# Decoder trunk on one core: rotation and key stacking rearranged, softmax from negated scores, probabilities scaled by a scalar per row

## The chip, the cores and the metric

The kernel runs on one core of one Trainium2 chip. The metric is the device time of one execution in microseconds; lower is better. The profile is one execution of the same program, recorded by the hardware profiler; its times are microseconds from its first instruction.

## What is computed

Two layers of a decoder trunk over 256 positions of width 1024, all in float32. Each layer is a half-step SwiGLU, a token mixer, and another half-step SwiGLU; a final RMSNorm ends it.

```
for l in range(2):
    x = x + 0.5 * swiglu(rms_norm(x, norm_ffn1[l]), ...)      # 1024 -> 2816 -> 1024
    x = x + hybrid_mixer(rms_norm(x, norm_mix[l]), ...)
    x = x + 0.5 * swiglu(rms_norm(x, norm_ffn2[l]), ...)
return rms_norm(x, norm_final)
```

The mixer has 8 NSA heads (in two groups that share keys; compressed, selected and window branches, which at 256 positions come to one causal softmax with two gates and one softmax over 15 compressed blocks) and 8 MoBA heads (one causal softmax each). Heads are 64 wide. Queries and keys get a partial rotation of their first 16 dimensions, and every softmax is masked, has its row maximum subtracted and its sum clamped at one:

```
x1 * cos - x2 * sin,  x2 * cos + x1 * sin                       # partial rotation
p = exp(s - max(s)); p / maximum(sum(p), 1.0)                   # masked softmax, s = q.k / 8
```

## The kernel before

Every weight block (128 x 1024) is streamed from HBM in the order of its use. Because the products are made of rounded float32 parts, each block is split in two: `whi`, a rounding copy on ScalarE (line 254), and `wlo`, the remainder, a subtraction on VectorE (line 283). Five raw and seven split buffers let this run ahead of TensorE; `st.pump()` and `st.split()` are the places in the program at which further blocks are split. Products are three matmuls (high by high, high by low, low by high).

The work is written out as one long program by hand, phase by phase: feed-forward, mixer, feed-forward, twice. Inside the mixer the order of calls (`m_feat("mk", 0)`, `nsa_s(0)`, `c_hidden()`, ...) interleaves three things: projections of MoBA keys, queries and values, NSA attention, and MoBA attention with the output projection. A scheduler then fixes the order on each engine from the program's order and its own estimates; at run time every engine goes through its queue in that fixed order and waits on semaphores.

The steps that the change touches, with their lines:

- Rotation. `rope_begin` (759) copies a projection from PSUM to SBUF on ScalarE (762), has ScalarE's queue issue two DMAs that bring the partner rows over into `SW` (763, 764; 16 rows each), and multiplies the projection by the cosines on VectorE (765). `rope_end` (767) multiplies `SW` by the signed sines and adds it to the result, both on GpSimd (768, 769). Both run seven times in a mixer: three times for NSA (queries, keys, queries), four times for MoBA.
- Key stacks. `stack_k` (798) and `m_stack` (1078) write a key's high part (ScalarE, 802 and 1086) and low part (VectorE, 803 and 1087) on 64 partitions; `repeat_k` (805) and `m_repeat` (1090) copy both to the other 64 partitions by DMAs from ScalarE's queue (807, 1093), two for NSA and four for MoBA in each mixer. `nsa_s` (1026) and `moba_s` (1188) need all 128 partitions.
- Softmax. `softmax` (976) scales, masks and takes the row maximum of scores in one VectorE instruction each (984, 985), negates the maxima (986), and lets ScalarE take the exponential with the sum (988, 989). `normalize` (992) works out the factor of each row on VectorE (994 to 998) and multiplies the probabilities by it on GpSimd (1000, 1001), with the factor read as a broadcast tensor.
- Values. The gates and the NSA values are evicted by ScalarE (1118, 1122), as are the MoBA values (1112), which `m_v` does after the last of its `st.pump()` calls; the four output accumulators (`out_block`, 1180; matmuls at 539 to 541) take over PSUM banks of tag `A`, which the MoBA values must leave first.

Of the kernel before, what the change touches and what calls it, by code (L numbers as in the profile page):

```python
# [133 lines left out]
def constants():  # L134
# [6 lines left out]
    for h in range(2):  # L141
        for d in range(half):
            C[h * 64 + 8 * d] = C[h * 64 + 8 * d + 4] = cos[:, d]
            Sg[h * 64 + 8 * d] = -sin[:, d]
            Sg[h * 64 + 8 * d + 4] = sin[:, d]
# [165 lines left out]
def trunk(ctx, tc, xin, wst, w1st, gains, glast, cst, small, out, phases=PHASES, n_raw=5, n_hl=7):  # L311
# [435 lines left out]
    def mixer(pi, l):  # L747
# [93 lines left out]
        rotk = rawk[:, 2:4]  # L841
        rs = state["rs"]
        rs8 = mp.tile([128, 2], F32, name="rs8", bufs=2)
        nrs = mp.tile([128, 2], F32, name="nrs", bufs=2)
        G.tensor_scalar(rs8, rs, DH ** -0.5, None, op0=OP.mult)
        G.tensor_scalar(nrs, rs, -1.0, None, op0=OP.mult)
        rope_begin(b1, rawq[:, 0:2], SW[:, 0:2], rotq[:, 0:2], con("C"))
# [21 lines left out]
        rope_begin(b2, rawk[:, 0:2], SW[:, 2:4], rotk, CK)  # L869
# [3 lines left out]
        rope_end(SW[:, 0:2], rotq[:, 0:2], con("Sg"))  # L873
# [4 lines left out]
        rope_begin(b3, rawq[:, 2:4], SW[:, 0:2], rotq[:, 2:4], con("C"))  # L878
        rope_end(SW[:, 2:4], rotk, SK)
# [3 lines left out]
        rope_end(SW[:, 0:2], rotq[:, 2:4], con("Sg"))  # L883
        repeat_k()
# [91 lines left out]
        def softmax(key, s1, s0, nb, gates):  # L976

            P = mp.tile([128, 3, 2, 128], F32, name="P", tag="P", bufs=3)[:, :, :nb]
            m = mp.tile([128, 2, nb], F32, name=f"mx{nb}", bufs=3)
# [3 lines left out]
            for r in range(nb):  # L983
                V.tensor_tensor_reduce(P[:, 0:2, r], s1[:, :, r], mk, rs8[:, 1:2], -3e38, OP.add, OP.max, m[:, 0, r:r + 1])
                V.tensor_tensor_reduce(P[:, 2, r], s0[:, r], m0, rs8[:, 0:1], -3e38, OP.add, OP.max, m[:, 1, r:r + 1])
            V.tensor_scalar(nm, m, -1.0, None, op0=OP.mult)
            for r in range(nb):
                A.activation(P[:, 0:2, r], P[:, 0:2, r], AF.Exp, bias=nm[:, 0, r:r + 1], accum_out=sm[:, 0, r:r + 1])
                A.activation(P[:, 2, r], P[:, 2, r], AF.Exp, bias=nm[:, 1, r:r + 1], accum_out=sm[:, 1, r:r + 1])
            PR[key] = (P, sm, nb, gates)  # L990

        def normalize(key):
# [63 lines left out]
        cur, ends, stacks, reps = {}, [], [], []  # L1056

        def m_feat(which, i):
# [5 lines left out]
            if i % 2 == 1:  # L1064
                h = i // 2
                raw = mp.tile([128, 2, S], F32, name="mraw", tag="F", bufs=2)
                tabs = (CK, SK) if which == "mk" else (con("C"), con("Sg"))
                sw, ro = SW[:, 2 * h:2 * h + 2], cur["rot"][:, 2 * h:2 * h + 2]
                rope_begin(cur["b"], raw, sw, ro, tabs[0])
# [264 lines left out]
```

## Time and profile before

| | |
|---|---|
| median of 3 runs | 1039.81 us (1039.14 to 1040.87) |
| the profiled execution's own time | 1037.38 us |
| its span, first to last instruction | 1035.6 us |
| TensorE busy | 1000.6 us (97%), 5861 matmuls |
| VectorE busy | 688.5 us (66%) |
| ScalarE busy | 593.3 us (57%) |
| GpSimd busy | 326.1 us (31%) |

1.8 us of the profiled execution's time lie outside its span. Engine names in the profile: PE is TensorE's matmul, PEld its weight load, DVE VectorE, ACT ScalarE, POOL GpSimd; a q behind an engine's name is its queue. The two mixers lie at about 197 to 340 us and 705 to 849 us. A matmul's end is modelled, so that neighbouring matmuls overlap in the records.

### The profile page before, as it was taken

The page shows a single profiled execution, that of the slowest core. Times are in us where ns is not written, and L with a number is a line of the kernel's source. Part 1 is how long each engine was busy: PE and PEld are TensorE (multiplying, and loading weights), DVE is VectorE, ACT ScalarE, POOL GpSimd, SP SyncE. Part 2 cuts the span into 40 slices and gives each one's busy share as a digit, 9 for nine tenths or more (in the row PEclk, how much of TensorE's full clock was granted, in tenths as well). Part 3 has the DMA queues.
Part 4 walks back from the last instruction along what each step waited for, and adds up shares of the span by engine and source line. Part 5 has one row for each costly group of instructions (what it writes and reads, how often), then busy time and mean ns, then how long its engine had stood idle before and what let it go on. Part 6 is the DMA issues. An engine that isn't in the chain of part 4 may idle for free.

```text
span 1035.6 us, 16186 instructions
## 1 busy us (share of the span) xinstructions
PE 1000.6 (97%) x5861; PEld 861.0 (83%) x5861; DVE 688.5 (66%) x1187; ACT 593.3 (57%) x1137; POOL 326.1 (31%) x425
## 2 busy tenths in 40 slices
PE   9999999998998999999999999999999989999997
PEld 7788888898776888888888888889888778888885
DVE  6766666589865766566676666566986648666664
ACT  6745555457766655555565555545677747555552
POOL 3622232145641422222232223121475313222230
PEclk9999999999999999999999999999999999999999
DMA  8685776455444466666556677764543426666531
GB/s 268 241 279 186 274 240 218 145 171 157 114 126 125 154 198 196 188 197 186 163 182 203 186 234 239 262 196 138 181 131 108 143 82 208 194 209 193 193 122 41
DMA packets 52848, 188.21 MB, mean 182 GB/s; under 512 B 6368, under 2 KB 6496, under 8 KB 51616
## 3 DMA queue, kind: packets, MB, share of 16 engines
q1 hardware_dynamic: 49680, 182.04, 55.4%
q10 hardware_dynamic: 3088, 5.14, 2.0%
q8 instruction: 46, 0.75, 0.3%
q14 instruction: 34, 0.28, 0.1%
HBM read 182.04 MB, written 1.05 MB: 177 GB/s over the span
## 4 chain that ended last, share of the span: by engine, by line
PE 83%; DVE 7%; ACT 5%; issue 2%; DMA 2%; POOL 1%; ACTq 0%; POOLq 0%; DVEq 0%
PE psB L560 15%; PE psA L539 9%; PE psA L540 9%; PE psA L541 9%; PE psB L562 8%; PE psD L560 8%; PE psC L560 7%; PE psD L562 4%; PE psC L562 4%; DVE wlo L283 3%; PE psA L533 2%; PE psA L532 2%; PE psA L534 2%; ACT whi L254 1%; PE psA L398 1%
## 5 line engine op out<-in xcount | busy, mean ns | idle before, releaser
L283 DVE TENSOR_TENSOR wlo<-wraw,whi 128x1024 fp32r<-128x1024 f32 x325 | 408.2, 1259 | 242.1 <-ACT whi L254 240.5
L254 ACT CAST whi<-wraw 128x1024 fp32r<-128x1024 f32 (+1 forms) x326 | 339.5, 1044 | 304.2 <-issue 175.4
L560 PE MATMUL psB<-x,whi 128*128 128x512 f32 x688 | 243.1, 394 | 3.4 <-DVE hs L627 3.3
L635 POOL TENSOR_TENSOR hs<-hs,rbc 128x256 f32<-128x256 f32 x88 | 75.0, 853 | 380.3 <-DVE hs L627 364.6
L562 PE MATMUL psB<-x,wlo 128*128 128x256 f32 x688 | 192.5, 280 | 0.0
L560 PEld LDWEIGHTS psB<-x,whi 128*128 128x128 f32 x688 | 129.2, 188 | 32.5 <-DVE hs L627 4.3
L541 PE MATMUL psA<-wlo,hp 128*128 128x512 f32 x352 | 136.9, 389 | 0.0
L540 PE MATMUL psA<-whi,hp 128*128 128x512 f32 x352 | 136.8, 389 | 0.0
L539 PE MATMUL psA<-whi,hp 128*128 128x512 f32 x352 | 136.2, 390 | 0.0
L562 PEld LDWEIGHTS psB<-x,wlo 128*128 128x128 f32 x688 | 129.4, 188 | 1.4
L637 POOL TENSOR_TENSOR hs<-hs,rbc 128x256 f32<-128x256 f32 x88 | 102.9, 1170 | 80.5 <-ACT hs L636 80.5
L560 PE MATMUL psC<-x,whi 128*128 128x512 f32 x352 | 124.9, 392 | 0.0
L560 PE MATMUL psD<-x,whi 128*128 128x512 f32 x352 | 124.8, 392 | 0.0
L562 PE MATMUL psC<-x,wlo 128*128 128x256 f32 x352 | 98.6, 280 | 0.9 <-DVE wlo L283 0.9
L562 PE MATMUL psD<-x,wlo 128*128 128x256 f32 x352 | 98.4, 280 | 0.0
L560 PEld LDWEIGHTS psC<-x,whi 128*128 128x128 f32 x352 | 66.1, 188 | 14.5
L560 PEld LDWEIGHTS psD<-x,whi 128*128 128x128 f32 x352 | 66.1, 188 | 14.4
L541 PEld LDWEIGHTS psA<-wlo,hp 128*128 128x128 f32 x352 | 66.1, 188 | 13.9
L539 PEld LDWEIGHTS psA<-whi,hp 128*128 128x128 f32 x352 | 66.0, 188 | 13.7
L540 PEld LDWEIGHTS psA<-whi,hp 128*128 128x128 f32 x352 | 66.1, 188 | 12.3
L532 PE MATMUL psA<-x,whi 128*128 128x256 f32 x256 | 72.8, 284 | 1.2 <-ACT PT L1010 0.8
L533 PE MATMUL psA<-x,whi 128*128 128x256 f32 x256 | 72.3, 283 | 0.7 <-DVE x L380 0.7
(229 smaller groups left out, 1586.3 us busy)
## 6 DMA issues: line engine op xcount, KB each, us to landing
wraw<-in_w SPq DMA_DIRECT2D x318, 512.0 KB, 4.3
W1a<-in_w SPq DMA_DIRECT2D x4, 1024.0 KB, 6.3
W1mixn<-in_w SPq DMA_DIRECT2D x2, 1024.0 KB, 7.6
W1late<-in_w SPq DMA_DIRECT2D x2, 1024.0 KB, 6.5
KM<-KM ACTq DMA_DIRECT2D x8, 256.0 KB, 3.2
wraw<-in_w SPq DMA_DIRECT2D x4, 420.0 KB, 3.7
wraw<-in_w SPq DMA_DIRECT2D x4, 256.0 KB, 5.1
X<-in_small SPq DMA_DIRECT2D x1, 1024.0 KB, 9.5
```

What stands on the lines that cost most here:

```text
L254: self.last_hi = self.nc.scalar.copy(hi[:, a:b], raw[:, a:b]).ins
L283: eng.tensor_sub(lo[:, :c], raw[:, :c], hi[:, :c].bitcast(F32))
L532: T.matmul(o, hi, xh, start=first, stop=False, skip_group_check=True)
L533: T.matmul(o, hi, xl, start=False, stop=False, skip_group_check=True)
L534: T.matmul(o, lo, xh, start=False, stop=last, skip_group_check=True)
L539: T.matmul(o, parts[:, 0, c], hi, start=first, stop=False, skip_group_check=True)
L540: T.matmul(o, parts[:, 1, c], hi, start=False, stop=False, skip_group_check=True)
L541: T.matmul(o, parts[:, 0, c], lo, start=False, stop=last, skip_group_check=True)
L560: T.matmul(o, blk128(hi, k), x.rearrange("p a t -> p (a t)"), start=k == 0, stop=k == KT - 1, skip_group_check=True)
L562: T.matmul(o[:, S:], blk128(lo, k), x[:, 0], start=False, stop=k == KT - 1, skip_group_check=True)
L635: G.tensor_mul(g, g, state["rbc"])
L637: G.tensor_mul(g, g, state["rbc5"])
```

## The change

1. The exponent's scale becomes -1 and the scores are scaled by the negative factor `nrs8` (a new tiny GpSimd instruction), so that the reduction is a minimum and gives the negated maximum; the instruction of line 986 goes.
2. The sine table changes sign and is applied before the rows are swapped: VectorE multiplies the projection by it from PSUM into `other`, the two DMAs swap rows of `other`, and `rope_end` is one addition on VectorE. The copy by ScalarE stays only for the two NSA query rotations of a mixer, whose unrotated queries are needed later, and comes behind the DMAs.
3. The key stacks are written to both halves of the partitions by ScalarE and VectorE; the six DMAs of a mixer and their calls go.
4. `normalize` uses an instruction with one tensor and a scalar per row on GpSimd.
5. One of the two evictions of NSA values and of MoBA values moves to VectorE, and those of MoBA come ahead of the last `st.pump()`.

```diff
-            Sg[h * 64 + 8 * d] = -sin[:, d]
-            Sg[h * 64 + 8 * d + 4] = sin[:, d]
+            Sg[h * 64 + 8 * d] = sin[:, d]
+            Sg[h * 64 + 8 * d + 4] = -sin[:, d]
...
-        def rope_begin(b, raw, sw, ro, ctab):
+        def rope_begin(b, raw, other, sw, ro, tabs):
             src = b.rearrange("p (a t) -> p a t", a=2)
-            A.copy(raw, src)
-            A.dma_start(sw[0:128:8], raw[4:128:8])
-            A.dma_start(sw[4:128:8], raw[0:128:8])
-            V.tensor_mul(ro, src, ctab[:, None, :].to_broadcast([128, 2, S]))
-
-        def rope_end(sw, ro, stab):
-            G.tensor_mul(sw, sw, stab[:, None, :].to_broadcast([128, 2, S]))
-            G.tensor_add(ro, ro, sw)
+            ctab, stab = (t[:, None, :].to_broadcast([128, 2, S]) for t in tabs)
+            V.tensor_mul(other, src, stab)
+            A.dma_start(sw[0:128:8], other[4:128:8])
+            A.dma_start(sw[4:128:8], other[0:128:8])
+            V.tensor_mul(ro, src, ctab)
+            if raw is not None:
+                A.copy(raw, src)
+
+        def rope_end(sw, ro):
+            V.tensor_add(ro, ro, sw)
...
                 src = rotk[half[g]].rearrange("p a (b t) -> p b a t", b=2)
-                A.copy(KK[g][half[g], 0], src)
-                V.tensor_sub(KK[g][half[g], 1], src, KK[g][half[g], 0].bitcast(F32))
-
-        def repeat_k():
-            for g in range(2):
-                A.dma_start(KK[g][half[1 - g]].bitcast(F32), KK[g][half[g]].bitcast(F32))
+                own = KK[g][half[g], 0]
+                for r in (half[g], half[1 - g]):
+                    A.copy(KK[g][r, 0], src)
+                for r in (half[g], half[1 - g]):
+                    V.tensor_sub(KK[g][r, 1], src, own.bitcast(F32))
...
-            m = mp.tile([128, 2, nb], F32, name=f"mx{nb}", bufs=3)
...
-                V.tensor_tensor_reduce(P[:, 0:2, r], s1[:, :, r], mk, rs8[:, 1:2], -3e38, OP.add, OP.max, m[:, 0, r:r + 1])
-                V.tensor_tensor_reduce(P[:, 2, r], s0[:, r], m0, rs8[:, 0:1], -3e38, OP.add, OP.max, m[:, 1, r:r + 1])
-            V.tensor_scalar(nm, m, -1.0, None, op0=OP.mult)
+                V.tensor_tensor_reduce(P[:, 0:2, r], s1[:, :, r], mk, nrs8[:, 1:2], 3e38, OP.add, OP.min, nm[:, 0, r:r + 1])
+                V.tensor_tensor_reduce(P[:, 2, r], s0[:, r], m0, nrs8[:, 0:1], 3e38, OP.add, OP.min, nm[:, 1, r:r + 1])
...
-                A.activation(P[:, 0:2, r], P[:, 0:2, r], AF.Exp, bias=nm[:, 0, r:r + 1], accum_out=sm[:, 0, r:r + 1])
+                A.activation(P[:, 0:2, r], P[:, 0:2, r], AF.Exp, scale=-1.0, bias=nm[:, 0, r:r + 1], accum_out=sm[:, 0, r:r + 1])
...
-                G.tensor_mul(P[:, 0:2, r], P[:, 0:2, r], sm[:, 0, r:r + 1, None].to_broadcast([128, 2, 128]))
-                G.tensor_mul(P[:, 2, r], P[:, 2, r], sm[:, 1, r:r + 1].to_broadcast([128, 128]))
+                G.tensor_scalar(P[:, 0:2, r], P[:, 0:2, r], sm[:, 0, r:r + 1], None, op0=OP.mult)
+                G.tensor_scalar(P[:, 2, r], P[:, 2, r], sm[:, 1, r:r + 1], None, op0=OP.mult)
...
             for a in range(2):
-                A.copy(K[half[a], :, a, 0], ro[half[a]])
-                V.tensor_sub(K[half[a], :, a, 1], ro[half[a]], K[half[a], :, a, 0].bitcast(F32))
-            reps.append(K)
-
-        def m_repeat():
-            K = reps.pop(0)
-            for a in range(2):
-                A.dma_start(K[half[1 - a], :, a].bitcast(F32), K[half[a], :, a].bitcast(F32))
+                own = K[half[a], :, a, 0]
+                for r in (half[a], half[1 - a]):
+                    A.copy(K[r, :, a, 0], ro[half[a]])
+                for r in (half[a], half[1 - a]):
+                    V.tensor_sub(K[r, :, a, 1], ro[half[a]], own.bitcast(F32))
...
+            if i == 3:
+                A.activation(MV[:, 0], cur["vb"][0], AF.Copy, scale=rs[:, 0:1])
+                V.tensor_scalar(MV[:, 1], cur["vb"][1], rs[:, 1:2], None, op0=OP.mult)
             st.pump()
-            if i == 3:
-                for blk in range(2):
-                    A.activation(MV[:, blk], cur["vb"][blk], AF.Copy, scale=rs[:, blk:blk + 1])
...
-        for blk in range(2):
-            A.activation(VN[:, blk], vb[blk][:, :S], AF.Copy, scale=rs[:, blk:blk + 1])
+        A.activation(VN[:, 0], vb[0][:, :S], AF.Copy, scale=rs[:, 0:1])
+        V.tensor_scalar(VN[:, 1], vb[1][:, :S], rs[:, 1:2], None, op0=OP.mult)
```

## Rows read from the trace of the kernel before

**Rows 1.** The page, section 4: the chain that ended last, by engine.

```profile
PE 83%; DVE 7%; ACT 5%; issue 2%; DMA 2%; POOL 1%; ACTq 0%; POOLq 0%; DVEq 0%
```

**Rows 2.** Stretches of mixer 1: length, busy us (instructions) per engine, clock, DMA.

```profile
214.00:237.00 23.00, 21.49 (x209) 19.50 (x209) 22.21 (x26) 13.55 (x23) 11.73 (x8) 1.00 0.62 184
237.00:268.00 31.00, 28.44 (x220) 25.57 (x219) 26.60 (x88) 22.27 (x67) 21.24 (x30) 1.00 0.51 149
268.00:297.00 29.00, 26.86 (x181) 22.69 (x179) 20.96 (x60) 22.38 (x61) 17.82 (x28) 1.00 0.35 97
```

**Rows 3.** Waits of TensorE, whole span: total us, times, longest us.

```profile
PE psA L539 <- ACT late L1112: 3.4, 2, 1.8
...
PE psB L1031 <- DVE qs L778: 2.8, 2, 1.5
...
PE psD L1048 <- ACT PcT L969: 2.1, 2, 1.0
PE psB L1031 <- DVE mx L984: 2.0, 2, 1.0
```

**Rows 4.** Key stack's DMAs (tile view), and ScalarE's timeline behind them.

```profile
DMA to landing us min/median/max: 4.9/5.3/5.4
...
231.18 2.19 ACTq L807 DMA_DIRECT2D KK<-KK  x2
233.41 0.41 ACT L776 CAST qs<-rotq 64x256 fp32r<-64x256 f32 x1 [2.48 <-DVE KK L803]
```

**Rows 5.** VectorE, 199 to 345 us, groups by form: busy us, mean ns, idle before.

```profile
L986 DVE TENSOR_SCALAR nm<-mx 128x4 f32<-128x4 f32 x8 | 3.1, 384 | 0.1
L803 DVE TENSOR_TENSOR KK<-rawk,KK 64x512 fp32r<-64x512 f32 x2 | 2.9, 1425 | 0.0
...
L765 DVE TENSOR_TENSOR rotq<-psA,const 128x512 f32<-128x512 f32 x2 | 1.4, 683 | 0.0
...
L283 DVE TENSOR_TENSOR wlo<-wraw,whi 128x560 fp32r<-128x560 f32 x1 | 0.7, 734 | 0.0
```

**Rows 6.** VectorE's timeline: two subtractions with GpSimd's rotation beside them, and without.

```profile
219.01 4.27 DVE L283 TENSOR_TENSOR wlo<-wraw,whi 128x1024 fp32r<-128x1024 f32 x2
...
227.09 2.36 DVE L283 TENSOR_TENSOR wlo<-wraw,whi 128x1024 fp32r<-128x1024 f32 x2
```

**Rows 7.** Busy us (instructions) in mixer 1: GpSimd's line 768, then line 769.

```profile
197.00:345.00 148.00, 10.71 (x7) 1.00 0.45 134
...
197.00:345.00 148.00, 11.25 (x7) 1.00 0.45 134
```

**Rows 8.** GpSimd, 199 to 345 us, groups by form; line 902 (ns min/median/max).

```profile
L1000 POOL TENSOR_TENSOR P<-P,sm 128x256 f32<-128x256 f32 x24 | 17.1, 712 | 29.0 <-DVE sm L996 16.2 <-DVE sm L998 4.3 <-ACT P L988 3.9
L1001 POOL TENSOR_TENSOR P<-P,sm 128x128 f32<-128x128 f32 x24 | 16.2, 677 | 0.0
...
L902 POOL TENSOR_SCALAR hxt<-hxt x2: 298/298/298, 240.6 to 749.2; 128x128 f32<-128x128 f32 x2
```

**Rows 9.** Who waited for the negated maxima (us, times), and one such wait.

```profile
  ACT P L988: 18.3, 13
...
264.25 0.51 ACT L988 ACTIVATE P<-P,nm 128x256 f32<-128x256 f32 x1 [3.47 <-DVE nm L986]
```

**Rows 10.** ScalarE's timeline at the MoBA values, and TensorE's first output matmul.

```profile
295.37 1.03 ACT L254 CAST whi<-wraw 128x1024 fp32r<-128x1024 f32 x1
296.30 0.68 ACT L1112 ACTIVATE late<-psA,ny 128x512 f32<-128x512 f32 x1
...
297.03 0.50 PE L539 MATMUL psA<-whi,mixn 128*128 128x512 f32 x1 [1.76 <-ACT late L1112]
```

**Rows 11.** Swapped rows: who waited for them (us, times), and the DMAs' landing.

```profile
  POOL SW L768: 24.7, 11
...
DMA to landing us min/median/max: 1.7/1.9/5.9
```

**Rows 12.** ScalarE, 199 to 345 us, groups by form: the copy of line 762.

```profile
L762 ACT COPY mraw<-psA 128x512 f32<-128x512 f32 x4 | 2.3, 576 | 0.0
```

More of the change, by code (lines that the diff above doesn't have):

```diff
@@ L840, in mixer @@
         rawq, rotq, rawk = RW("rawq"), RW("rotq"), RW("rawk")
-        rotk = rawk[:, 2:4]
+        other, rotk = rawk[:, 0:2], rawk[:, 2:4]
         rs = state["rs"]
         rs8 = mp.tile([128, 2], F32, name="rs8", bufs=2)
+        nrs8 = mp.tile([128, 2], F32, name="nrs8", bufs=2)
         nrs = mp.tile([128, 2], F32, name="nrs", bufs=2)
         G.tensor_scalar(rs8, rs, DH ** -0.5, None, op0=OP.mult)
+        G.tensor_scalar(nrs8, rs, -DH ** -0.5, None, op0=OP.mult)
         G.tensor_scalar(nrs, rs, -1.0, None, op0=OP.mult)
-        rope_begin(b1, rawq[:, 0:2], SW[:, 0:2], rotq[:, 0:2], con("C"))
+        rope_begin(b1, rawq[:, 0:2], other, SW[:, 0:2], rotq[:, 0:2], (con("C"), con("Sg")))
         st.pump()
@@ L868, in mixer @@
                     V.tensor_mul(Fk[kv][par * 64:(par + 1) * 64, :, g * NC_:(g + 1) * NC_], blocks(src), blocks(rb))
-        rope_begin(b2, rawk[:, 0:2], SW[:, 2:4], rotk, CK)
+        rope_begin(b2, None, other, SW[:, 2:4], rotk, (CK, SK))
         st.pump()
@@ L872, in mixer @@
         feature_one(b3[:, :S], st.use("in", l, 2), True)
-        rope_end(SW[:, 0:2], rotq[:, 0:2], con("Sg"))
+        rope_end(SW[:, 0:2], rotq[:, 0:2])
         for r in (0, 1):
@@ L877, in mixer @@
         feature_one(b3[:, S:], st.use("in", l, 3), False)
-        rope_begin(b3, rawq[:, 2:4], SW[:, 0:2], rotq[:, 2:4], con("C"))
-        rope_end(SW[:, 2:4], rotk, SK)
+        rope_begin(b3, rawq[:, 2:4], other, SW[:, 0:2], rotq[:, 2:4], (con("C"), con("Sg")))
+        rope_end(SW[:, 2:4], rotk)
         stack_k()
@@ L882, in mixer @@
         nsa_v(0)
-        rope_end(SW[:, 0:2], rotq[:, 2:4], con("Sg"))
-        repeat_k()
+        rope_end(SW[:, 0:2], rotq[:, 2:4])
         nsa_v(1)
@@ L983, in softmax @@
             for r in range(nb):
-                V.tensor_tensor_reduce(P[:, 0:2, r], s1[:, :, r], mk, rs8[:, 1:2], -3e38, OP.add, OP.max, m[:, 0, r:r + 1])
-                V.tensor_tensor_reduce(P[:, 2, r], s0[:, r], m0, rs8[:, 0:1], -3e38, OP.add, OP.max, m[:, 1, r:r + 1])
-            V.tensor_scalar(nm, m, -1.0, None, op0=OP.mult)
+                V.tensor_tensor_reduce(P[:, 0:2, r], s1[:, :, r], mk, nrs8[:, 1:2], 3e38, OP.add, OP.min, nm[:, 0, r:r + 1])
+                V.tensor_tensor_reduce(P[:, 2, r], s0[:, r], m0, nrs8[:, 0:1], 3e38, OP.add, OP.min, nm[:, 1, r:r + 1])
             for r in range(nb):
-                A.activation(P[:, 0:2, r], P[:, 0:2, r], AF.Exp, bias=nm[:, 0, r:r + 1], accum_out=sm[:, 0, r:r + 1])
-                A.activation(P[:, 2, r], P[:, 2, r], AF.Exp, bias=nm[:, 1, r:r + 1], accum_out=sm[:, 1, r:r + 1])
+                A.activation(P[:, 0:2, r], P[:, 0:2, r], AF.Exp, scale=-1.0, bias=nm[:, 0, r:r + 1], accum_out=sm[:, 0, r:r + 1])
+                A.activation(P[:, 2, r], P[:, 2, r], AF.Exp, scale=-1.0, bias=nm[:, 1, r:r + 1], accum_out=sm[:, 1, r:r + 1])
             PR[key] = (P, sm, nb, gates)
@@ L1055, in mixer @@
         MV = late[:, 512:1536].rearrange("p (b c) -> p b c", b=2)
-        cur, ends, stacks, reps = {}, [], [], []
+        cur, ends, stacks = {}, [], []
         def m_feat(which, i):
@@ L1065, in m_feat @@
                 h = i // 2
-                raw = mp.tile([128, 2, S], F32, name="mraw", tag="F", bufs=2)
                 tabs = (CK, SK) if which == "mk" else (con("C"), con("Sg"))
                 sw, ro = SW[:, 2 * h:2 * h + 2], cur["rot"][:, 2 * h:2 * h + 2]
-                rope_begin(cur["b"], raw, sw, ro, tabs[0])
-                ends.append((which, h, sw, ro, tabs[1]))
+                rope_begin(cur["b"], None, mp.tile([128, 2, S], F32, name="rots", tag="F", bufs=2), sw, ro, tabs)
+                ends.append((which, h, sw, ro))
             st.pump()
@@ L1075, in m_end @@
             rope_end(*e[2:])
-            stacks.append(e[:2] + e[3:4])
+            stacks.append(e[:2] + e[3:])
         def m_stack():
@@ L1149, in mixer @@
         nsa_s(4)
-        m_repeat()
         nsa_pv(0)
@@ L1217, in mixer @@
         m_end()
-        m_repeat()
         moba_s(0)
```

## The prediction

> **What bounds the kernel now.** I read the page first, then the busy time by stretch, TensorE's waits, the two tiles that the change takes DMAs from, the groups of VectorE, GpSimd and ScalarE, and last the timelines around each wait. The chain that ended last runs through TensorE for 83% of the span [rows 1]: the kernel is bound by matmuls, and only time in which TensorE stands still can be won. The change touches the mixers alone. In the stretches of mixer 1 that hold everything it touches, TensorE stands still for 1.5 of 23, 2.6 of 31 and 2.1 of 29 us [rows 2], 6.2 us, or 12.4 us for two mixers. That is the ceiling for a change that removes no matmul. In the same rows VectorE is busy for 22.2 of 23, 26.6 of 31 and 21.0 of 29 us, GpSimd for 11.7, 21.2 and 17.8: VectorE is the next bound, and the change moves work to it.
>
> Four waits make up most of that stillness [rows 3], each once in a mixer: the first output matmul on the MoBA values (3.4 us in all), NSA's first scores on what is named `qs` (2.8), a matmul on `PcT` (2.1), scores on a PSUM bank that the maxima of line 984 have to leave (2.0). Together 10.3 us.
>
> **Part by part: the load.** What lies off TensorE costs only through those waits, so I first ask whether VectorE can carry what it is given.
>
> - GpSimd loses the rotation: 10.7 us in line 768 and 11.3 in line 769, 22.0 us a mixer, 14 instructions [rows 7].
> - VectorE gets a second multiplication from PSUM for each rotation, at 0.68 us [rows 5], and an addition of 128x512. No such addition from SBUF is in the trace; the nearest is the subtraction of 128x560 at 0.73 us [rows 5], which I take, between 0.68 (the PSUM form) and 2.1 (half of 4.27 us for a double-width subtraction beside GpSimd [rows 6]).
> - The key stacks: two more subtractions for NSA and four for MoBA in a mixer, of 64x512, between 0.73 us (the clean one) and 1.43 us (what `KK` pays now) [rows 5]. ScalarE gets six more copies of 64x512 at about 0.58 us and loses five rotation copies at 0.58 [rows 12]; that cancels. The DMAs that go were issued by ScalarE, and each waited there for VectorE's subtraction: the pair of `KK` held ScalarE's queue from 231.2 to 233.4 us, 2.48 us without work, with the next query stack and, behind it, the table of exponentials queued [rows 4].
> - The seven remaining pairs of row-swap DMAs now wait in ScalarE's queue for a VectorE multiplication instead of ScalarE's own copy. What queues behind is the same mixture of splits and exponentials. Seven new waits against six that go: I count nothing for the balance.
> - The negations go: eight of four columns cost 3.1 us of VectorE in mixer 1 [rows 5].
> - Evictions: one of NSA and one of MoBA values, 0.68 us each at most [rows 5].
> - Two extra tiny GpSimd instructions for `nrs8` lie in the mixers' openings, where GpSimd has no other work to hand on; nothing.
>
> In the 23 us VectorE gets two multiplications (1.4; the first rotation's lies before 214 us), three additions (2.2) and two subtractions (1.5 to 2.9): 5.1 to 6.5 us. Some comes back, because GpSimd's rotation slowed VectorE: two `wlo` subtractions took 4.27 us with it beside them and 2.36 without [rows 6], 1.9 us, and the two `KK` subtractions can fall from 1.43 to 0.73, 1.4 us. Net 1.8 to 3.2 us on 22.2. In the other 60 us: four multiplications (2.7), four additions (2.9), four subtractions (2.9 to 5.7) and two evictions (1.4), less 3.1 for the negations: 6.8 to 9.6 on 47.6. Over 83 us VectorE goes from 69.8 to between 78.4 and 82.6 us, 80.5 in the middle. It fits, and leaves 2.5 us in the middle by which each mixer's 83 us may shrink, a little more if splits slip behind 297 us: about 3 us a mixer, 6 in all.
>
> **Part by part: the waits.**
>
> - `qs` (2.8 us): the named releaser is not the last. Both `KK` DMAs were issued at 231.2 us or later and took 5.3 us to land [rows 4], so the first scores could not start before about 236.5; I read this wait as the DMA's. Without it the next thing late is VectorE's own queue, up by 1.8 to 3.2 us ahead of the key's low parts. Between 0 and 2.8; I take 1.6.
> - `PcT` (2.1 us): ScalarE stood for 3.47 us before the exponentials at 264.25 us, because the negation was queued on VectorE behind other work; in all, exponentials waited 18.3 us for negations, 13 times [rows 9]. `PcT`'s copy is queued behind these exponentials. Without the negation the exponential waits for the reduction itself, which ends earlier; what is late next is the reduction, behind the added subtractions. Between 0 and 2.1; I take 1.3.
> - Maxima (2.0 us): a VectorE queue that is late because ScalarE was late. The 2.48 us on ScalarE go, the added VectorE work comes. Between a loss of 2 and 2.0; I take 0.7.
> - MoBA values (3.4 us): the eviction started at 296.30 us behind a split copy of 1.03, and TensorE followed at 297.03 [rows 10]. Ahead of the pump it starts a split earlier, and VectorE takes the other half. Between 1.0 a mixer and all; I take 2.6 of 3.4.
>
> Sum 1.6 + 1.3 + 0.7 + 2.6 = 6.2 us, which agrees with the 6 that VectorE's load leaves. The profiled execution's 1037.4 us (span 1035.6 and 1.8 around it) become 1031.2. The median of the runs lies 2.4 above that execution: 1039.8 - 6.2 = 1033.6 us.
>
> **GpSimd's scaling.** Now 0.71 and 0.68 us for 256 and 128 columns, 24 of each in a mixer [rows 8]. The form with a scalar per row is not in the trace; the nearest, with constants, takes 0.30 for 128 columns [rows 8], at most 0.6 for 256. That is the lower end; the upper one is twice today's, 1.4. I take 0.3 for 128 and 0.6 for 256, since these lie nearest in form. It shortens GpSimd's work by up to 0.4 us a pair, and none of the four waits is on GpSimd: nothing in the sum.
>
> **Rivals.**
>
> - VectorE becomes the bound. If nothing comes back from GpSimd's absence, its load in the 83 us is 69.8 + 6.5 + 9.6 = 85.9 us; each mixer then takes 2.9 us longer and wins nothing: 1039.8 + 5.8 = 1045.6 us. It decides from a net addition of 13.2 us a mixer on. For it: 22.2 of 23 us today. Against it: the 1.9 us of rows 6. The Trainium skill (SBUF — State Buffer, "Who interferes with whom") says that a VectorE instruction with two SBUF inputs contends with a GpSimd instruction that reads SBUF, whichever issues first blocking the other for its whole length; rows 6 agree. By that rule the new additions and subtractions contend with the scaling that stays on GpSimd, so that their prices lie toward the upper ends and the load toward 82.6 us of 83, with next to nothing won in the stretch.
> - The addition waits for its rows on VectorE. GpSimd waited 24.7 us in 11 waits for swapped rows, whose DMAs land after 1.9 us in the middle and 5.9 at worst [rows 11]; there nobody else was queued. On VectorE, maxima and `wlo` stand behind. If half of it shows on TensorE, 12.3 us against the 6.2 won: 1045.9. It decides when more than 6.2 of the 24.7 show. Against it: most landings are near 1.9, and an order with other work between hides that.
> - The waits only move. TensorE's next instructions wait for whatever is then last, and the gain is eaten: 1039.8.
> - All of the ceiling: VectorE's relief is large, and the small waits go too: 1039.8 - 12.4 = 1027.4.
> - The new GpSimd form costs 1.4 us: then a pair of rows takes 5.6 us from exponential to transposition instead of 2.8. Each of the 16 NSA rounds has other work to cover it, but if 0.2 of each extra 2.8 showed in 16 rounds, 9 us less the 6.2: 1042.6.
>
> **How the numbers follow.** A difference of 0.2%, 2 us, is about what a measurement here can tell from none. Forecast, 1033.6 (its own range 1029 to 1037.5): 0.45. All of the ceiling: 0.14. The waits only move: 0.15, of which 0.12 within 2 us of before and 0.03 faster. VectorE the bound: 0.14. The row waits: 0.08. The GpSimd form: 0.04. So faster 0.45 + 0.14 + 0.03 = 0.62, same 0.12, slower 0.26. The range reaches from the ceiling's case with its spread to both slower cases near 1046: 1025 to 1046; beyond lie some 0.05 below and 0.12 above.
>
> **What the new profile would show.** Right: no wait of NSA's first scores over 0.5 us; exponentials start within 0.3 us of the reduction's end; the first output matmul waits under 0.5 us; `wlo` subtractions at 214 to 237 us take about 1.2 us each; VectorE is busy for 78 to 83 of the former 83 us. Wrong: VectorE stands waiting for DMAs into `SW`; waits on maxima (line 984 or 985) above 2 us a mixer; scalings by row slower than 0.7 us. The prediction is wrong above all if the order of the engines' queues, which the scheduler lays anew, puts an addition or a low part in front of the maxima that TensorE's PSUM banks wait for.

## The result, and the profile after

The changed kernel takes 1048.55 us in the median of 4 runs (1047.55 to 1051.06), the kernel before 1040.34 in the runs beside it (1039.14 to 1041.76): a ratio of 1.008, 95% interval 1.0063 to 1.0098. Forecast were 1033.6 us and a range up to 1046. It is slower, and outside the range.

The page of the changed kernel first: busy time by engine, and the chain that ended last.

```profile
PE 1011.7 (96%) x5861; PEld 872.2 (83%) x5861; DVE 696.0 (66%) x1199; ACT 596.7 (57%) x1135; POOL 313.1 (30%) x399
PE 84%; DVE 8%; issue 3%; ACT 2%; DMA 1%; POOL 1%; ACTq 0%; DVEq 0%
```

The chain still runs through TensorE, as in [rows 1]. To find the loss I cut out both mixers, from the first transposition behind the norm to the same one of the next phase: first the kernel before, then the changed one (length, busy us by engine with instructions, then clock, DMA share, GB/s).

```profile
200.50:331.20 130.70, 121.98 (x899) 105.21 (x897) 96.74 (x239) 84.21 (x204) 63.24 (x92) 1.00 0.48 141
709.10:840.20 131.10, 122.43 (x899) 105.42 (x897) 95.97 (x239) 84.19 (x204) 61.84 (x88) 1.00 0.46 141
sum 261.80, PE 244.41 PEld 210.63 DVE 192.71 ACT 168.40 POOL 125.08; mean PE 122.20 PEld 105.32 DVE 96.35 ACT 84.20 POOL 62.54
```

```profile
202.80:339.80 137.00, 127.14 (x899) 110.04 (x897) 100.18 (x245) 85.88 (x203) 56.81 (x79) 0.95 0.39 121
717.60:853.30 135.70, 125.92 (x899) 109.06 (x897) 100.30 (x245) 85.89 (x203) 55.88 (x75) 0.96 0.39 122
sum 272.70, PE 253.06 PEld 219.09 DVE 200.47 ACT 171.76 POOL 112.69; mean PE 126.53 PEld 109.55 DVE 100.24 ACT 85.88 POOL 56.34
```

The mixers grew by 272.70 - 261.80 = 10.9 us. TensorE stands still in them for 272.70 - 253.06 = 19.6 us against 17.4, only 2.2 more. The other 8.7 us are matmuls: the same 899 in each mixer are busy for 253.06 us instead of 244.41, because the granted clock is 0.95 and 0.96 instead of 1.00. Of the rest of the profiled execution's surplus (span 1049.3 against 1035.6), 2.3 us lie ahead of the first mixer, where nothing was changed; the other executions of the changed kernel have spans of 1045.8 to 1046.9. The two profiled executions lie at the ends of what was measured: over all executions on record the mean granted clock of the kernel before is 0.989 to 0.999, 0.994 in the median and 0.999 in the profiled one, while the changed kernel's four have 0.983 (the profiled one), 0.986, 0.986 and 0.989. The clock's 8.7 us are those of this pair; that the changed kernel has the lower clock holds for the medians too.

TensorE's waits, the answer to [rows 3] (total us, times, longest):

```profile
PE psA L970 <- DVE Pc L964: 9.1, 2, 4.6
PE psB L560 <- DVE hs L627: 3.3, 3, 1.1
PE psB L1033 <- DVE nm L987: 3.1, 2, 1.6
PE psB L1033 <- DVE sm L996: 2.9, 2, 1.5
...
PE psA L540 <- DVE mixm L1025: 1.7, 4, 0.5
PE psC L1035 <- ACT hid L892: 1.2, 2, 0.6
```

Three of the four waits of [rows 3] are gone. The fourth, for the bank that NSA's maxima must leave, has grown. The fourth scores of mixer 1, in the kernel before:

```profile
243.58 0.70 PE L1031 MATMUL psB<-KK,qs 128*128 128x512 f32 x2 [1.00 <-DVE mx L984]
```

The third and the fourth in the changed kernel:

```profile
244.51 0.70 PE L1033 MATMUL psB<-KK,qs 128*128 128x512 f32 x2 [1.55 <-DVE nm L987]
247.00 1.19 PE L1033 MATMUL psB<-KK,qs 128*128 128x512 f32 x2 [1.47 <-DVE sm L996]
```

The third scores did not wait before; the fourth wait 1.5 us instead of 1.0 (VectorE's row behind the maxima, `sm`, gives the wait its name). Together they are 6.0 us in the two mixers, where there were 2.0: VectorE starts the first maxima only at 243.56 us, behind four query low parts, a weight's low part, the gates and the moved eviction. New is `Pc`, the compressed branch's probabilities (4.6 us in each mixer; 0.3 in all before). The wait for `hs` lies outside the mixers. What the clock does behind these waits, in stretches of mixer 1:

```profile
244.00:248.00 4.00, 2.02 (x7) 1.43 (x8) 4.00 (x14) 3.58 (x13) 1.66 (x5) 0.76 0.56 162
248.00:252.00 4.00, 4.00 (x21) 4.00 (x19) 3.28 (x12) 2.39 (x11) 3.70 (x4) 0.50 0.42 134
252.00:272.00 20.00, 17.66 (x144) 16.40 (x143) 17.93 (x52) 14.65 (x37) 13.07 (x15) 0.98 0.32 104
272.00:282.00 10.00, 7.75 (x40) 7.25 (x41) 8.56 (x25) 6.97 (x21) 4.95 (x5) 0.66 0.21 60
```

After two stops near 1.5 us within 4 us, the clock stands at 0.50, the lower level of 1.2 GHz, while TensorE is busy in all of 248 to 252; after the stop of 4.6 us it falls again. In the stretches of [rows 2] it was 1.00 throughout.

Why `Pc` is late is read from the queues. VectorE (start, us), from the branch's first scaling to its last multiplication (line 964):

```profile
259.95 0.58 DVE L943 SCALAR_TENSOR_TENSOR Pc<-psA,rs,const 128x128 f32<-128x128 f32 x2
...
261.87 0.69 DVE L764 TENSOR_TENSOR rots<-psA,const 128x512 f32<-128x512 f32 x1
262.47 0.69 DVE L767 TENSOR_TENSOR rotmq<-psA,const 128x512 f32<-128x512 f32 x1
263.06 0.41 DVE L947 TENSOR_REDUCE mc<-Pc 128x16 f32<-128x256 f32 x1
...
268.33 0.38 DVE L956 TENSOR_REDUCE mc<-Pc 128x16 f32<-128x256 f32 x1
268.75 0.52 DVE L781 TENSOR_TENSOR qs<-rotmq,qs 64x256 fp32r<-64x256 f32 x1
...
271.19 0.69 DVE L764 TENSOR_TENSOR rots<-psA,SK 128x512 f32<-128x512 f32 x1
271.80 0.68 DVE L767 TENSOR_TENSOR rotmq<-psA,CK 128x512 f32<-128x512 f32 x1
272.40 0.24 DVE L961 SCALAR_TENSOR_TENSOR mc<-mc,GT 128x8 f32<-128x8 f32 x2
272.55 1.22 DVE L283 TENSOR_TENSOR wlo<-wraw,whi 128x1024 fp32r<-128x1024 f32 x1
273.69 0.42 DVE L964 TENSOR_TENSOR Pc<-Pc,mc 128x256 f32<-128x256 f32 x1
```

GpSimd in between:

```profile
262.05 0.92 POOL L1002 TENSOR_SCALAR P<-P,sm 128x256 f32<-128x256 f32 x1 [1.74 <-DVE sm L1000]
262.95 0.60 POOL L1003 TENSOR_SCALAR P<-P,sm 128x128 f32<-128x128 f32 x1
263.53 1.87 POOL L1002 TENSOR_SCALAR P<-P,sm 128x256 f32<-128x256 f32 x1
265.38 0.60 POOL L1003 TENSOR_SCALAR P<-P,sm 128x128 f32<-128x128 f32 x1
265.95 0.62 POOL L950 TENSOR_TENSOR Pc<-Pc,mc 128x256 f32<-128x256 f32 x1
```

A rotation's two multiplications stand in front of the reduction (line 947), four scalings in front of GpSimd's subtraction (line 950), and four query low parts, the next rotation and a weight's low part in front of the last multiplication. The instructions of the branch itself take under half a microsecond each on VectorE.

### The profile page after: what moved, and what is told of

It is laid out like the page before. It is cut to its first block, busy times and chain, and to the rows that moved or that the text cites. A ratio compares the mean times of both kernels' runs of the same rounds, so it can differ in the third digit from the quotient of the medians.

```text
span 1049.3 us, 16141 instructions
## 1 busy us (share of the span) xinstructions
PE 1011.7 (96%) x5861; PEld 872.2 (83%) x5861; DVE 696.0 (66%) x1199; ACT 596.7 (57%) x1135; POOL 313.1 (30%) x399
## 4 chain that ended last, share of the span: by engine, by line
PE 84%; DVE 8%; issue 3%; ACT 2%; DMA 1%; POOL 1%; ACTq 0%; DVEq 0%
PE psB L560 15%; PE psA L540 9%; PE psA L541 9%; PE psA L539 9%; PE psD L560 8%; PE psB L562 7%; PE psC L560 7%; PE psD L562 4%; PE psC L562 4%; DVE wlo L283 3%; PE psA L533 2%; PE psA L532 2%; PE psA L534 2%; PE psA L1010 1%; ACT whi L254 1%
## 5 line engine op out<-in xcount | busy, mean ns | idle before, releaser
L283 DVE TENSOR_TENSOR wlo<-wraw,whi 128x1024 fp32r<-128x1024 f32 x325 | 400.1, 1234 | 247.9 <-ACT whi L254 245.8
L1002 POOL TENSOR_SCALAR P<-P,sm 128x256 f32<-128x256 f32 x48 | 56.4, 1175 | 69.9 <-DVE sm L998 39.9
L533 PE MATMUL psA<-x,whi 128*128 128x256 f32 x256 | 74.9, 292 | 0.7 <-DVE x L380 0.7
```

What stands on the lines that cost most here:

```text
L283: eng.tensor_sub(lo[:, :c], raw[:, :c], hi[:, :c].bitcast(F32))
L533: T.matmul(o, hi, xl, start=False, stop=False, skip_group_check=True)
L1002: G.tensor_scalar(P[:, 0:2, r], P[:, 0:2, r], sm[:, 0, r:r + 1], None, op0=OP.mult)
```

## The experiments

Each ratio is against the kernel before, in 5 rounds, with its 95% interval; a permil is a thousandth of that kernel's time. The change falls into five parts: negated scores, rotation, key stacks, scaling, evictions. The versions with scaling, negated scores or key stacks alone also carry one moved line, the reservation of the tile `mraw`, which now stands behind two lines that only name tables and slices.

**One part alone.** Scaling:

```diff
-                G.tensor_mul(P[:, 0:2, r], P[:, 0:2, r], sm[:, 0, r:r + 1, None].to_broadcast([128, 2, 128]))
...
+                G.tensor_scalar(P[:, 0:2, r], P[:, 0:2, r], sm[:, 0, r:r + 1], None, op0=OP.mult)
...
```

> The kernel before with the fourth part alone: GpSimd scales the probabilities by a scalar per row. Theory A (the new GpSimd form takes 0.92 and 0.60 us where the old one took 0.61 and 0.40, and makes the compressed branch's probabilities late, for which TensorE stood 4.6 us a mixer and then ran at a lower clock): 1045 to 1050 us, with a wait of TensorE for the tile Pc of 3 us or more in each mixer. Theory B (VectorE's added multiplications and additions of the rotation make them late): 1039 to 1042 us, no such wait.

Measured: 0.9969 (0.9954 to 0.9983). The new form is slower (the last section has the numbers) and the kernel faster: the form is not the cause. Why it is 3 us faster was not found; its executions had a granted clock of 0.996 in the median, the kernel before beside them 0.993.

Rotation, with its sine product ahead of the swap:

```diff
+            V.tensor_mul(other, src, stab)
+            A.dma_start(sw[0:128:8], other[4:128:8])
...
-            G.tensor_add(ro, ro, sw)
+            V.tensor_add(ro, ro, sw)
```

> The kernel before with the second part alone: the sine product on VectorE ahead of the row swap, and the addition on VectorE. Theory A (GpSimd's new scaling form is the cause): 1034 to 1040 us, as GpSimd gives up 22 us a mixer. Theory B (VectorE's load): 1045 to 1050 us with a wait for Pc of 3 us or more a mixer.

Measured: 0.998 (0.9966 to 0.9994). The largest wait is for the DMA of `KK`: 9.4 us in all, 4.8 at most. The key stack is late: in mixer 1 its second subtraction ends at 234.8 us instead of 232.9, and its DMAs take 7.0 us to land instead of 5.3. Theory B falls for the rotation by itself.

Negated scores:

```diff
+                V.tensor_tensor_reduce(P[:, 0:2, r], s1[:, :, r], mk, nrs8[:, 1:2], 3e38, OP.add, OP.min, nm[:, 0, r:r + 1])
-            V.tensor_scalar(nm, m, -1.0, None, op0=OP.mult)
```

> The kernel before with the first part alone: scores scaled by the negative factor, minimum instead of maximum, no negation. Theory C (rotation and key stacks together fill VectorE's queue, through which the compressed branch's probabilities pass five times): 1034 to 1041 us. Theory D (the negated scores put the reductions in another order, and TensorE waits for PSUM banks): 1043 us or more, with the two waits of 1.5 us for psB that the three kernels with this part showed.

Measured: 0.9985 (0.9976 to 0.9994). Theory D falls.

Key stacks:

```diff
+                for r in (half[g], half[1 - g]):
+                    V.tensor_sub(KK[g][r, 1], src, own.bitcast(F32))
...
-                A.dma_start(KK[g][half[1 - g]].bitcast(F32), KK[g][half[g]].bitcast(F32))
```

> The kernel before with the third part alone: key stacks written by ScalarE and VectorE, no DMA. Both theories: the wait of 2.8 us for the first scores goes, 1036 to 1041 us. Theory C also: VectorE's queue is later by the six subtractions, but alone they make no wait for Pc over 1 us.

Measured: 1.0015 (1.0004 to 1.0026). TensorE no longer waits for the keys, but 6.8 us for maxima and 2.0 for `Pc`.

So three parts are faster by themselves and one hardly slower; the evictions were not run alone. The loss is in how the parts meet.

**Several parts together.** The change without the scaling, and without scaling and rotation:

```diff
...
-                G.tensor_scalar(P[:, 2, r], P[:, 2, r], sm[:, 1, r:r + 1], None, op0=OP.mult)
...
+                G.tensor_mul(P[:, 2, r], P[:, 2, r], sm[:, 1, r:r + 1].to_broadcast([128, 128]))
```

> The changed kernel with the old scaling on GpSimd (everything but the fourth part). Theory A (scaling form): 1032 to 1037 us, about the forecast of 1033.6, granted clock back at 0.99 or more. Theory B (VectorE's load): 1045 to 1049 us, the wait for Pc still there.

> The changed kernel without the second and the fourth part: negated scores, key stacks without DMA and the moved evictions alone. Theory A (scaling form): within 3 us of the run without the scaling, 1032 to 1038 us. Theory B (VectorE's load): 1032 to 1038 us, and 8 us or more below the run that keeps the rotation on VectorE.

Measured: 1.0101 (1.0084 to 1.0117), with 9.9 us of waits for `Pc`; and 1.003 (1.002 to 1.0041), 1043.44 us, with none for `Pc`. Theory A falls. The rotation, faster alone, costs 7 permil here; but the second version, which both theories had put at 1032 to 1038 us, is slower than the kernel before as well, with the waits for NSA's maxima at 6.0 us. Rotation and stacks by themselves:

```diff
+            V.tensor_mul(other, src, stab)
...
+                    V.tensor_sub(KK[g][r, 1], src, own.bitcast(F32))
```

> The kernel before with the second and the third part. Theory C: 1046 to 1052 us, with a wait for Pc of 3 us or more in each mixer, although neither part alone has it. Theory D: 1034 to 1041 us and no wait for Pc, since the scores are not negated.

Measured: 1.0039 (1.0025 to 1.0053), 1044.28 us, with 5.2 us of waits for `Pc`: between the ranges of C and D. The two should have cancelled by their own ratios.

The change without the key stacks, without the evictions, and without both:

```diff
...
-        A.activation(VN[:, 0], vb[0][:, :S], AF.Copy, scale=rs[:, 0:1])
-        V.tensor_scalar(VN[:, 1], vb[1][:, :S], rs[:, 1:2], None, op0=OP.mult)
+        for blk in range(2):
+            A.activation(VN[:, blk], vb[blk][:, :S], AF.Copy, scale=rs[:, blk:blk + 1])
```

> The changed kernel with the key stacks of before: copies and subtractions on the own half only, the other half by DMA; negated scores, rotation, scaling and evictions stay changed. Theory E (the key stacks without DMA are what turns the change: they put six subtractions on VectorE and six copies on ScalarE in front of maxima and of the compressed branch's subtraction): the parts that were faster alone add up, -1.5, -2.0 and -3.1 permil, so 0.992 to 0.997 of before; the wait for Pc under 1 us in all, no stretch of 4 us at a granted clock below 0.7 in mixer 1; a wait on KK's DMA of 3 to 9 us comes back. Rival F (any shift of so much work from GpSimd and DMA to VectorE makes the chains late, whichever part): 1.002 to 1.008, and Pc or maxima still wait 3 us or more.

> The changed kernel with the evictions of both mixers' values as before (both on ScalarE, MoBA's behind the pump). Rival G (VectorE's half of NSA's values eviction stands in front of the first maxima and makes them late): 0.998 to 1.003, the waits for maxima at 244 and 247 us shorter by 0.7 us each, and the wait for MoBA's values of 3.4 us back. Theory E: the evictions carry little, 1.006 to 1.010, with the wait for Pc left.

> Before with negated scores, rotation and scaling alone; stacks and evictions as before. Theory E: the three gains add, 0.993 to 0.996 (1033 to 1036 us), the fastest of all so far. Rival F: they do not add, 0.998 to 1.004, with a new wait on VectorE of 3 us or more in the trace.

Measured: 1.0033 (1.0014 to 1.0051) without stacks, 4.4 us of waits for `Pc`; 1.0058 (1.0038 to 1.0078) without evictions, 8.2 us; and 0.9966 (0.9953 to 0.998), 1036.9 us, without both, with 0.5 us of waits for `Pc` and 8.4 for `KK`; this one is called the fast version below. Theory E, the stacks alone, falls: the evictions cost as well. Rival F held for the version without stacks, which fell into its range, but falls with the fast version: those three parts together are faster, though by 3.4 permil, not the 6.6 of their sum.

Then each half of a part. NSA's stack by DMA, MoBA's stack by DMA, and NSA's stack added to the fast version:

```diff
+            for a in range(2):
+                A.dma_start(K[half[1 - a], :, a].bitcast(F32), K[half[a], :, a].bitcast(F32))
```

> The changed kernel with only NSA's key stack (KK) filled by DMA as before; MoBA's stack stays without DMA. If theory E holds by NSA's half (first scores come early, VectorE has not cleared its queue, maxima late, then TensorE stands and its clock falls): 0.995 to 1.000, the waits on nm and sm at 244 to 247 us gone. If it is MoBA's half (four subtractions and four copies in front of Pc): 1.006 to 1.010, with the Pc wait of 9 us left.

> The changed kernel with MoBA's key stacks filled by DMA as before; NSA's stack stays without DMA. With NSA's half by DMA the time stayed at 1.0086, so the stacks' share of the loss (0.5% here) should be MoBA's four copies and four subtractions in a mixer: 1.001 to 1.005, Pc wait at 4.4 us or less as without any stack. If neither half alone brings it back: 1.006 to 1.010, and it is VectorE's sum.

> Negated scores, rotation, scaling and NSA's key stack without DMA; MoBA's stack and the evictions as before. Against negated_rotation_scaling (0.9966) it takes away a wait of 8.4 us for KK's DMA and adds two subtractions and two copies of 64x512 in a mixer. If that half of the stack is harmless: 0.990 to 0.995, the fastest version. If early first scores only meet a VectorE that has not cleared its queue: 0.996 to 1.001, with waits for nm and sm of 1.5 us each at the first scores and the clock at half behind them.

Measured: 1.0086 (1.0067 to 1.0106), 1.001 (0.9995 to 1.0025), and 0.9965 (0.995 to 0.998), 1036.76 us. In this company MoBA's four subtractions and copies carry 7 permil, NSA's nothing: added to the fast version they take away 8.4 us of waits for `KK` and put 5.1 us of waits for NSA's maxima in their place. And NSA's eviction added to the fast version:

```diff
-        for blk in range(2):
-            A.activation(VN[:, blk], vb[blk][:, :S], AF.Copy, scale=rs[:, blk:blk + 1])
+        A.activation(VN[:, 0], vb[0][:, :S], AF.Copy, scale=rs[:, 0:1])
+        V.tensor_scalar(VN[:, 1], vb[1][:, :S], rs[:, 1:2], None, op0=OP.mult)
```

> Negated scores, rotation and scaling, and of the evictions NSA's alone (its second half on VectorE); MoBA's behind the pump on ScalarE as before; stacks by DMA. With both evictions the time was 1.0033, without 0.9966. If NSA's eviction in front of the first maxima is the one that costs: 1.001 to 1.005, with a wait for Pc of 2 us or more in each mixer. If it is MoBA's: 0.995 to 0.999 and no wait for Pc over 1 us.

Measured: 1.0046 (1.003 to 1.0062): 8 permil for one instruction of 0.48 us in each mixer that replaces one on ScalarE. `Pc` is waited for 4.2 us again, `KK` 11.7 instead of 8.4. Its own 0.48 us cannot explain that. The scores of the compressed branch start 3.2 and 1.1 us later in the two mixers than in the fast version; the wait for `KK`, 7.0 and 4.7 us instead of 4.2 each, is 2.8 and 0.5 of that. From these scores to `Pc` it takes 14.7 us instead of 13.1. Which of the moved instructions did it was not tried.

**The chain of `Pc`.** Its use on TensorE put later, behind the last MoBA key projection:

```diff
-        c_transpose()
         nsa_s(4)
-        nsa_pv(0)
...
         m_feat("mk", 3)
+        c_transpose()
+        nsa_pv(0)
```

> The changed kernel with two calls moved: the transposition of the compressed branch's probabilities and the first NSA output come behind the next scores and the next key projection, so that TensorE has some 9 us of other work meanwhile. If the wait for Pc and the lower clock behind it are what costs (theories C and D alike): 1033 to 1041 us, one fall of the granted clock a mixer less. If VectorE's load as a whole is the bound, whatever order TensorE has: 1046 us or more, the wait showing up elsewhere.

Measured: 1.011 (1.0097 to 1.0123); TensorE then waits for NSA's maxima and sums instead (6.4 and 5.1 us), and the clock is 0.60 from 272 to 280 us. By its own expectation this spoke for VectorE's load as the bound; the run with the order alone, below, speaks against it. The chain's subtraction given to VectorE:

```diff
-            G.tensor_sub(flat, flat, mb)
+            V.tensor_sub(flat, flat, mb)
```

> The changed kernel with one edit: the subtraction of the maxima in the compressed branch (Pc minus mc) goes from GpSimd to VectorE. In the changed kernel that subtraction ran 2.9 us after the reduction before it, because GpSimd's queue had scalings in front. Theory H (the chain of Pc is the cause: it ends 4.6 us late, TensorE stands, the clock falls): Pc is ready 2.5 to 3 us earlier in the mixer, the wait for Pc falls from 9.1 to 2 to 4 us in all, the low clock behind it shortens, and the time falls by 5 to 10 us to 1.000 to 1.004. Rival I (VectorE is late as a whole and Pc only shows it): the subtraction costs VectorE 0.3 us or more in front of other work, the wait for Pc stays above 7 us or goes to the next instruction of VectorE, and the time stays within 2 us of the changed kernel, 1.006 to 1.010.

Measured: 1.0084 (1.0069 to 1.0099), the wait for `Pc` 9.2 us. The subtraction ran 0.4 us earlier in the mixer, `Pc` no earlier at all: what stands ahead of the last multiplication sets it. Theory H falls in this form.

Last, the order alone. Every operation of the changed kernel stays; two calls are only held back in VectorE's queue:

```diff
...
-        m_feat("mq", 1)
+        with tc.issue_after(cmp_["top"].ins):
+            m_feat("mq", 1)
...
-        m_feat("mk", 3)
+        with tc.issue_after(cmp_["mul"].ins):
+            m_feat("mk", 3)
```

> The changed kernel with every operation unchanged; two calls are only pinned in VectorE's queue: the rotation of the first MoBA queries behind the compressed branch's reduction of maxima, the rotation of the second MoBA keys behind its last multiplication. Theory J (the order of the queues makes the chain late): from the scores to Pc 11 to 13 us instead of 17.3, the wait for Pc falls from 9.1 to under 3 us in all, no stretch at half clock at 274 to 281 us, and 5 to 10 us of the loss come back: 0.999 to 1.004. Rival I (too much work for VectorE in whatever order): the chain is early but the maxima and scalings behind it are late by as much, TensorE waits 4 us or more a mixer elsewhere in that stretch, and the time stays at 1.006 to 1.011.

Measured: 1041.42 us, 1.0009 (1.0 to 1.0018). VectorE's and GpSimd's rows of this kernel, its two stretches around them, and what is left of TensorE's waits:

```profile
254.92 0.62 POOL L950 TENSOR_TENSOR Pc<-Pc,mc 128x256 f32<-128x256 f32 x1
```

```profile
260.23 0.41 DVE L956 TENSOR_REDUCE mc<-Pc 128x16 f32<-128x256 f32 x1
...
263.56 0.41 DVE L964 TENSOR_TENSOR Pc<-Pc,mc 128x256 f32<-128x256 f32 x1
```

```profile
248.00:262.00 14.00, 14.00 (x117) 13.05 (x117) 13.39 (x45) 11.41 (x31) 11.82 (x12) 1.00 0.27 81
262.00:275.00 13.00, 12.66 (x106) 11.50 (x102) 12.04 (x30) 9.78 (x30) 6.16 (x8) 1.00 0.40 128
```

```profile
PE psB L1033 <- DVE nm L987: 3.1, 2, 1.6
PE psB L1193 <- DVE nm L987: 3.1, 2, 1.6
PE psB L1033 <- DVE sm L996: 2.9, 2, 1.5
```

The first compressed scores of the three kernels, the kernel before first, the changed one, this one, and the last multiplication of the kernel before:

```profile
248.91 1.87 PE L936 MATMUL psA<-KC,rawq 128*128 128x32 f32 x16
```

```profile
256.47 1.86 PE L939 MATMUL psA<-KC,rawq 128*128 128x32 f32 x16
```

```profile
250.77 1.87 PE L939 MATMUL psA<-KC,rawq 128*128 128x32 f32 x16
```

```profile
261.30 0.42 DVE L961 TENSOR_TENSOR Pc<-Pc,mc 128x256 f32<-128x256 f32 x1
```

From the first compressed score to the last multiplication this kernel takes 263.56 - 250.77 = 12.8 us, as the kernel before (261.30 - 248.91 = 12.4); the changed one took 273.69 - 256.47 = 17.2. TensorE is busy for 26.66 of these 27 us at full clock, with VectorE busy for 25.4 of them. Theory J holds for this wait, and rival I falls: 7 of the 8 permil come back with no work removed. The waits for NSA's maxima stay, and MoBA's scores (line 1193) wait twice for maxima, 3.1 us in all. Behind the pair of waits for NSA's maxima, 1.6 and 1.5 us in either mixer, the clock differs from mixer to mixer:

```profile
242.00:252.00 10.00, 8.16 (x64) 7.69 (x65) 9.12 (x36) 8.88 (x27) 5.94 (x10) 1.00 0.32 107
752.00:756.00 4.00, 2.96 (x12) 2.80 (x13) 3.58 (x17) 3.36 (x11) 3.12 (x7) 0.50 0.45 148
```

The profiled execution is the fastest of this kernel's eleven.

The same idea for NSA's maxima, on the fast version with NSA's stack: the gates, two query stacks and the weight splits of one call held back behind them, and the two rotations as above.

```diff
+        with tc.issue_after(cmp_["low", 0].ins):
+            st.pump()
...
+        with tc.issue_after(cmp_["low", 0].ins):
+            V.tensor_scalar(GT, GT, 1.0, None, op0=OP.add)
+            V.reciprocal(GT, GT)
             for r in (2, 3):
                 stack_q(rotq[:, r], r)
```

> Negated scores, rotation, scaling and NSA's key stack without DMA (0.9965 without pins); MoBA's stack and the evictions as before. Pinned in VectorE's queue: the gates, the second pair of query stacks and the weight splits of the first MoBA key call behind the first maxima of NSA; the rotations of the first MoBA queries and second MoBA keys behind the compressed branch, as in the run before. Theory J (order): the waits on nm and sm of NSA's first scores fall from 5.1 to under 2 us in all, nothing of that size takes their place, 0.990 to 0.995, the fastest. Rival I (VectorE has no room in the opening in whatever order): what is pushed back makes the next maxima or weight splits late, 0.996 to 1.001.

Measured: 1.0072 (1.0058 to 1.0085), outside both ranges. The maxima started at 35.4 us of the mixer instead of 40.3, and the two waits at line 1033 are gone; 2.2 us for maxima at line 1035 and 2.7 for `Pc` are left, and one is new:

```profile
PE psA L923 <- POOL gh L911: 9.0, 2, 4.5
```

The compression's matmuls (line 923) now stand right behind the third scores, with the fourth moved behind them (256.1 us instead of 246.5 in mixer 1), and TensorE waits for `gh` from GpSimd, whose first two instructions towards it (lines 904 and 905) took 2.6 us instead of 0.7. The order changed once more, and another chain was late; whether a better order exists for these waits stays open. The fastest versions are the ones at 0.9966 and 0.9965; the scaling alone, at 0.9969, is as fast within its interval.

## Why the prediction was wrong

**The step that failed is the sum of the waits.** It let four waits of [rows 3] shrink, each in the order of the old queues, and added 1.6 + 1.3 + 0.7 + 2.6. Three did go, and whole: 8.3 us, where 5.5 had been taken for them. The fourth term, the maxima, was taken as a gain of 0.7 and bounded by "a loss of 2"; the wait went from 2.0 to 6.0 us, a loss of 4.0, although ScalarE's 2.48 us in front of it went as forecast. And what was late next was bounded only at those four places: `Pc`, which did not show in [rows 3], had no term and went from 0.3 to 9.1 us. The text named the danger in its last sentence, an order laid anew, and gave it no price and no chance. The run with only the order changed shows that the order in front of `Pc` was 7 of 8 permil.

**The clock was no term.** Stops were priced at their own length. In the mixers TensorE stood 2.2 us longer and its matmuls ran 8.7 us longer. The waits of [rows 3] took 1.0 to 1.8 us each, with the clock at 1.00; those of the changed kernel come as a pair of 1.5 and as one of 4.6, with the clock at 0.50 behind them. Nearly the same idle time went with far more matmul time. That the spread of the stops alone does this is not shown: the same pair left the clock at 1.00 in the first mixer of the run with only the order changed and at 0.50 in its second.

**VectorE's load was mis-sized, to the safe side.** The stretches of [rows 2], in the changed kernel (its mixer starts 2.3 us later):

```profile
214.00:237.00 23.00, 23.00 (x224) 21.23 (x223) 20.48 (x30) 12.04 (x20) 1.44 (x2) 1.00 0.56 188
237.00:268.00 31.00, 27.39 (x198) 25.26 (x197) 27.69 (x79) 24.47 (x67) 15.89 (x20) 0.89 0.38 120
268.00:297.00 29.00, 24.41 (x163) 21.13 (x162) 23.63 (x69) 20.49 (x56) 22.66 (x26) 0.88 0.29 82
```

That is 71.8 us where 78 to 83 were forecast. Part of it is that these stretches hold less of the slower kernel's work, 585 matmuls instead of 610; the kernel with only the order changed, at full clock there with 617, has 74.0 us. Over the whole mixer the load rose by (200.47 - 192.71) / 2 = 3.9 us, not by the 8.6 to 12.8 of the two sums (1.8 to 3.2 and 6.8 to 9.6). The relief was larger than taken: in 214 to 297 us the mean `wlo` fell from 1.42 to 1.22 us, the `KK` subtraction from 1.43 [rows 5] to 0.69. The Trainium skill (SBUF — State Buffer, "Who interferes with whom") lets a VectorE instruction with two SBUF inputs contend with a GpSimd instruction that reads SBUF; that the later one is blocked for the other's whole length it says of VectorE's two-port modes. The shorter `wlo` agrees; the upper prices that the prediction drew from that rule did not come. The rival "VectorE becomes the bound" thus ended near the measured time (1045.6) by a mechanism that the trace does not show: VectorE had 11 us to spare in the 83 (9 with only the order changed) and was late only at two places, for what stood in front.

**The other rivals.** The addition does not wait for its rows as GpSimd did [rows 11]: VectorE stood 5.5 us in 5 waits for `SW`, most of it before the first scores. The new GpSimd form takes 0.92 us in the median and 1.18 in the mean, above the 0.6 taken and below the 1.4 feared, and the part alone is faster; its gain "up to 0.4 us a pair" adds up to 0.5 by the prediction's own prices, and the sum held nothing for it. "The waits only move" is the right family, but it ended at no change; it took no account of the clock.

**What was right.** `KK`'s DMA was the true releaser behind `qs`: with the key stacks alone, no wait for `qs` or `KK` is left, and with the rotation alone the wait carries the DMA's name. The first scores no longer wait for queries or keys (0.6 us a mixer for `hid` came instead), and `wlo` subtractions take about 1.2 us. Exponentials follow the reduction more closely: 10.6 us in 20 waits, 0.5 each, against 1.4 each [rows 9]. All three signs listed as "wrong" showed: VectorE waiting for `SW` (5.5 us), maxima above 2 us a mixer (3.0), and scalings above 0.7.

## What to carry to other kernels

Where a scheduler fixes each engine's queue, a diff changes the order of everything near it, and a part's gain alone says little about its gain in company: look at what stands in front of each short chain that TensorE will need, and pin that order before judging the parts. Price a stop of TensorE with a range for what its clock loses behind it, read from stretches of the same kernel: the same pair of stops cost nothing in one mixer and some 3 us in the other (an estimate from 4 us at 0.50 and 4 at 0.66). The waits to fear are not in the old list; they are the chains with the least slack behind engines that receive work.

## What was not expected of the hardware

GpSimd's multiplication by a scalar per row is slower than the one by a broadcast tensor. The kernel before and the changed one (duration min/median/max in ns):

```profile
L1000 POOL TENSOR_TENSOR P<-P,sm x48: 603/612/1602, 246.1 to 831.0; 128x256 f32<-128x256 f32 x48
L1001 POOL TENSOR_TENSOR P<-P,sm x48: 389/400/1382, 246.6 to 831.6; 128x128 f32<-128x128 f32 x48
```

```profile
L1002 POOL TENSOR_SCALAR P<-P,sm x48: 917/924/2278, 248.3 to 843.9; 128x256 f32<-128x256 f32 x48
L1003 POOL TENSOR_SCALAR P<-P,sm x48: 595/604/1822, 249.2 to 844.8; 128x128 f32<-128x128 f32 x48
```

The Trainium skill (GPSIMD Engine Reference, section 4.1, "Engine selection") calls GpSimd about twice as slow as VectorE for two inputs and roughly at line rate for one. Here the form with one tensor input takes half as long again as the one with two, 0.92 against 0.61 us; the measurement decides.

The second is the clock: matmuls of 256 columns followed each other every 0.12 us before the stop at 270 us and every 0.21 us at 279 us, with the granted clock at 0.50 in 248 to 252 us although TensorE was busy in every slice of it. In the changed kernel a lower clock followed the stop of 4.6 us and the pair of 1.5 us each, in both mixers. The length of a stop alone doesn't tell the price. The pair left 1.00 in one mixer and 0.50 in the other with only the order changed. The fast version stops for 4.2 us for `KK` in each mixer; its mixers' clocks are 0.99 and 0.97, and behind the second of these stops the clock stood at 0.50 in 748 to 752 us as well. What sets it stays open.
